# Half-size products of gate and up: four raw weight buffers for two, nine split pairs for ten, six ordinary pairs in front

## The chip, the core and the metric

The kernel runs on one core of a Trainium2 chip. The metric is device time in microseconds (us) of one execution; before the change it is 1347.97 us, the median of three runs (1345.63 to 1348.08).

## What is computed

Two transformer blocks, one after the other, on 512 tokens of 1024 features in float32. The change lies in the feed-forward part of the first block:

```python
h = rms_norm(x, ln_pre_ffn[l])
f = (jax.nn.silu(h @ w_gate[l]) * (h @ w_up[l])) @ w_down[l]
x = x + rms_norm(f, ln_post_ffn[l])
```

`w_gate` and `w_up` are 1024 x 2816 each, `w_down` is 2816 x 1024. Ahead of it stands a mixing layer (dilated attention and pooling), behind it the second block with another mixing layer, a second feed-forward part and a gated output.

## The kernel before

**Split operands.** TensorE (PE) multiplies in a reduced-precision form of float32 (fp32r). To keep accuracy every operand is split in two: `hi` is a rounded copy, written by ScalarE (ACT), and `lo` is what the rounding left, value minus `hi`, written by VectorE (DVE). `mm3` (L185) then makes three matmuls of each product: hi by hi (L188), hi by lo of the other side (L189), lo by hi (L190). A split weight tile of 128 x 512 is a *split pair* (`wh`, `wl` in the profile); `NW` = 10 of them exist. Weights come from memory by DMA, issued by SP, into *raw* buffers (`wr`, up to 128 x 1048 float32); the pool `wts` (L71) holds two.

**The pairs.** Gate and up are made in 22 pairs of output blocks, 128 gate columns and the 128 up columns beside them. The first `PLAIN` = 5 pairs are ordinary: each block is a slab of 8 k-tiles x 3 matmuls with 512 columns (tokens), so 48 matmuls a pair. The other 17 pairs are made by Strassen's scheme in Winograd's form: the weights of a pair are four pieces (gate and up, each with an upper and a lower half of the 1024 features), the activations four quarters (two feature halves, two token halves), and seven half-size products do for eight. A half-size product is 4 k-tiles x 3 matmuls of 256 columns, so a pair takes 84 matmuls of 256. The price is preparation.

- *Of the activations, once:* `h_forms` (L719) makes seven operands out of the four quarters: scaled quarters (L738), sums and differences (L747), and the split of each (L177, L178, L180, L181). These are 15 steps, run after ordinary pair 1, 2 and 3, five at a time (L660 to L665).
- *Of the weights, per pair:* `w_forms` (L762) loads the two raw tiles (L767), makes four sums (L774) and splits seven operands (ACT at L782, DVE at L783).

In the half-size loop (L669 on) the products are named by their number j: 0 to 4 are made in the pair's turn, 5 (`left`) and 6 (`right`) are put off into the next pair's turn. DVE combines the results: L693 needs product 3, L697 needs 4, L701 needs 5, L705 needs 6; L707 and the split at L180/L181 finish the activation.

**What sets the order.** The code names dependencies only; the instructions of each engine are put in their order when the program is built, by a planner that plays the program on a model of the engines. On the chip each engine then runs its queue in that order, and waits by semaphores. So a change of buffer counts alters the order everywhere. A tile whose buffer is in use waits for the last reader of the tile before it: a raw tile for the last ACT or DVE operation that reads it, a split pair for the last matmul.

Of the kernel before, what the change touches and what calls it, by code (L numbers as in the profile page):

```python
# [26 lines left out]
GATE = 5  # L27
GATE2 = 4
WARM = 10
NW = 10  # L30
BANKS = (3, 2, 2, 1)
SHARE = 4
ORDER1 = (
# [9 lines left out]
DONE2 = [0, 1, 2, 3, 4, 5, 6, 7]  # L43
KA2 = 6
BESIDE = 4
PLAIN = 5
NA2 = 4
SLOTS = dict(h=16, o=14, k=16, z=6, v=8, p=8, t=6, m=8)

# [13 lines left out]
class Builder:  # L63
    def __init__(self, ctx, tc, io):
        self.tc = tc
        self.nc = tc.nc
        self.io = io
        self.n = 0
        pool = lambda name, bufs, **k: ctx.enter_context(tc.tile_pool(name=name, bufs=bufs, **k))
        self.cp = pool("const", 1)  # L70
        self.wp = pool("wts", 2)  # L71
        self.sp = pool("slots", 1)
        self.mp = pool("small", 8)
        self.dp = pool("dram", 1, space=bass.MemoryType.DRAM)
        psum = dict(space=bass.MemoryType.PSUM)
        self.pd = pool("psd", BANKS[0], **psum)
        self.pS = pool("pss", BANKS[1], **psum)
        self.pT = pool("pst", BANKS[2], **psum)
        self.pV = pool("psv", BANKS[3], **psum)
        self.cyc = 0  # L80
        self.nlo = 0
        self.share = 0
# [68 lines left out]
    def wunit(self, name, u, parts=2, pieces=1):  # L151
# [9 lines left out]
        for i in range(parts):  # L161
            c = raw[:, i * w:i * w + w]
            hi = self.wp.tile([P, WH], F32R, tag="hi", name=self.nm("wh"), bufs=NW)
            lo = self.wp.tile([P, WH], F32R, tag="lo", name=self.nm("wl"), bufs=NW)
            nc.scalar.activation(hi[:, :w], c, AF.Copy)  # L165
# [466 lines left out]
    def ffn1(self, h, R):  # L632
        nc = self.nc
        self.tables("silu_and_others")
        get = self.units("w_gu1")
        self.parked = self.dp.tile([KD, P, S], F32, tag="parked", name="parked")
        for m in range(KD):
            nc.sync.dma_start(self.parked[m], self.res[m])
        act = []
        todo = []  # L640
        for i in range(PLAIN):
            if i == 0:
                early = [self.psum(True) for _ in range(BESIDE)]
                self.beside(early, range(BESIDE), h, ((0, 256), (256, S)), get)
            gu = []
            for s in (2 * i, 2 * i + 1):
                if s < BESIDE:
                    gu.append(early[s])
                    continue
                gu.append(self.psum(True))  # L650
                self.slab(gu[-1], "w_gu1", s, h, units=get)
            g, u = gu
            t = self.slot("z")
            nc.vector.tensor_tensor(t, g, R, ALU.mult)
            self.act(t, t, AF.Silu)
            w = self.slot("z")
            nc.vector.tensor_tensor(w, u, R, ALU.mult)
            nc.vector.tensor_tensor(t, t, w, ALU.mult)
            act.append(self.split(t, **self.act_tiles1(i)))
            if i == 0:  # L660
                forms, todo = self.h_forms(R)
                each = -(-len(todo) // (PLAIN - 2))
            else:
                for step in todo[(i - 1) * each:i * each]:
                    step()  # L665
        self.res = None
        sums = [self.slot("m") for _ in range(4)]
        late = []
        for i in range(PLAIN, KF):  # L669
            wf = self.w_forms(2 * i, sums)  # L670
            A, B, C = (self.psum(True) for _ in range(3))
            half = slice(0, 256)
            e, f, t = self.slot("z"), self.slot("z"), self.slot("z")

            def times(out, j, first=False, wf=wf):
                hi, lo = wf(j)
                for k in range(4):
                    c = slice(k * P, k * P + P)
                    a = slice(k % 2 * 256, k % 2 * 256 + 256)
                    bh, bl = forms[j][k // 2]  # L680
                    self.mm3(out[:, half], hi[:, c], lo[:, c], bh[:, a], bl[:, a], first and k == 0, k == 3, True)

            times(A, 0, True)
            nc.scalar.activation(e[:, half], A[:, half], AF.Copy)
            times(C, 1, True)
            for step in late[:1]:
                step()
            times(A, 2)
            nc.scalar.activation(e[:, 256:], A[:, half], AF.Copy)
            for step in late[1:]:  # L690
                step()
            times(B, 3, True)
            nc.vector.tensor_tensor(t[:, half], B[:, half], e[:, half], ALU.add)  # L693
            self.act(t[:, half], t[:, half], AF.Silu)
            times(A, 4)
            nc.scalar.activation(f[:, half], A[:, half], AF.Copy)
            nc.vector.tensor_tensor(f[:, 256:], C[:, half], f[:, half], ALU.add)  # L697

            def left(A=A, t=t, times=times):
                times(A, 5)  # L700
                nc.vector.tensor_tensor(t[:, half], t[:, half], A[:, half], ALU.mult)  # L701

            def right(C=C, t=t, e=e, f=f, times=times, i=i):
                times(C, 6)
                nc.vector.tensor_tensor(t[:, 256:], C[:, half], e[:, 256:], ALU.add)  # L705
                self.act(t[:, 256:], t[:, 256:], AF.Silu)
                nc.vector.tensor_tensor(t[:, 256:], t[:, 256:], f[:, 256:], ALU.mult)  # L707
                act.append(self.split(t, -1.0, **self.act_tiles1(i)))
            late = [left, right]
        for step in late:  # L710
            step()
        self.tables("natural_log_exp_and_others")
        return self.post(act, None, "w_down", "ln_post_ffn", "ln_mix_2", False)
# [48 lines left out]
    def w_forms(self, u, sums):  # L762
# [15 lines left out]
        for j, f in enumerate(src):  # L778
            c = f()
            hi = self.wp.tile([P, WH], F32R, tag="hi", name=self.nm("wh"), bufs=NW)  # L780
            lo = self.wp.tile([P, WH], F32R, tag="lo", name=self.nm("wl"), bufs=NW)
            nc.scalar.activation(hi[:, :512], c, AF.Copy)  # L782
# [423 lines left out]
```

## Time and profile before

| | us |
|---|---|
| median of three runs | 1347.97 |
| the profiled execution's own time | 1350.33 |
| its span (first to last instruction) | 1348.5 |
| PE busy in the span | 1302.2 |
| DVE busy | 937.3 |
| ACT busy | 724.0 |
| POOL busy | 153.5 |

The page gives busy time per engine, the span in 40 slices, and the chain of work that ended last, followed backwards from the last instruction. The trace behind it can be asked for single stretches: busy time and granted clock of TensorE in a window, the instructions in order of time, and who waited for whom. A matmul's duration in the trace is longer than the distance to the next, since matmuls overlap; what a stream of them costs is read from start to start. Below, the half-size stage is the stretch from 295.68 us (first half-size matmul) to 485.04 us (first matmul of `w_down`).

### The profile page before, as it was taken

Reading aid. Unit: us, or ns where it says so; the run is one execution under the profiler, and the core shown is the slowest. Engines: PE = TensorE matmul, PEld = TensorE weight load, DVE = VectorE, ACT = ScalarE, POOL = GpSimd, SP = SyncE. Lnnn points to the kernel's source line nnn. Section 1 sums busy time; section 2 is a strip of 40 time slices with the busy share of each in tenths; the row PEclk is TensorE's granted clock in tenths of the full one; section 3 lists DMA queues with packets and bytes.
Section 4 is the critical chain, followed back from the end, with each engine's and each line's share of the span. In section 5 each row is a group of like instructions: output and inputs, shape, how many; then the busy total and the mean of one; then the engine's idle time right before and its main releaser. Section 6 shows DMA issues by size and latency. Waiting matters only on the chain.

```text
span 1348.5 us, 21638 instructions
## 1 busy us (share of the span) xinstructions
PE 1302.2 (97%) x8062; PEld 1156.7 (86%) x8062; DVE 937.3 (70%) x1962; ACT 724.0 (54%) x1460; POOL 153.5 (11%) x190
## 2 busy tenths in 40 slices
PE   9799999989999999999999999999999999999998
PEld 9799979868999988888989999788888888888887
DVE  6777985898888863228688878766887777733354
ACT  6466745655555653227577777754554444522241
POOL 1233320000000000001223334430000000000000
PEclk9999999999999999999999999999999999999999
DMA  6322333412222363227334444224322222222221
GB/s 226 113 63 68 95 103 117 135 38 95 95 95 95 102 212 110 94 78 224 129 106 117 124 115 137 79 95 150 115 97 97 99 96 94 102 94 94 94 79 63
DMA packets 51114, 145.99 MB, mean 108 GB/s; under 512 B 6497, under 2 KB 7393, under 8 KB 51009
## 3 DMA queue, kind: packets, MB, share of 16 engines
q1 hardware_dynamic: 51008, 144.62, 33.4%
q8 instruction: 63, 1.03, 0.3%
q14 instruction: 43, 0.34, 0.1%
HBM read 124.47 MB, written 8.39 MB: 99 GB/s over the span
## 4 chain that ended last, share of the span: by engine, by line
PE 69%; DVE 20%; DMA 7%; issue 2%; ACT 2%; SPq 0%; POOL 0%; DVEq 0%; ACTq 0%; POOLq 0%
PE p L188 16%; PE p L190 16%; PE p L189 16%; DMA wr<-in_w_gu 5%; PE p L374 5%; PE p L375 5%; PE p L376 4%; DVE wl L783 4%; DVE sm L774 3%; DVE wl L168 2%; PE p L285 2%; PE p L294 1%; PE p L293 1%; PE p L263 1%; DVE sp L267 1%
## 5 line engine op out<-in xcount | busy, mean ns | idle before, releaser
L168 DVE TENSOR_TENSOR wl<-wr,wh 128x512 fp32r<-128x512 f32 x332 | 237.4, 727 | 200.6 <-ACT wh L165 193.3
L165 ACT ACTIVATE wh<-wr 128x512 fp32r<-128x512 f32 (+1 forms) x349 | 215.8, 629 | 294.4 <-PE p L189 237.6
L188 PE MATMUL p<-sh,wh 128*128 128x512 f32 (+1 forms) x768 | 260.3, 343 | 10.7 <-ACT wh L782 10.1
L190 PE MATMUL p<-sh,wl 128*128 128x512 f32 (+1 forms) x768 | 263.9, 345 | 2.9 <-DVE wl L783 2.4
L189 PE MATMUL p<-sh,wh 128*128 128x512 f32 (+1 forms) x768 | 261.3, 342 | 0.0
L374 PE MATMUL p<-wh,sh 128*128 128x256 f32 (+1 forms) x672 | 193.2, 289 | 6.8 <-ACT sz L488 3.8
L375 PE MATMUL p<-wl,sh 128*128 128x256 f32 (+1 forms) x672 | 191.8, 286 | 0.2
L376 PE MATMUL p<-wh,sh 128*128 128x256 f32 (+1 forms) x672 | 190.9, 286 | 0.0
L188 PEld LDWEIGHTS p<-sh,wh 128*128 128x128 f32 x768 | 144.3, 189 | 31.1 <-ACT wh L782 12.5
L190 PEld LDWEIGHTS p<-sh,wl 128*128 128x128 f32 x768 | 145.7, 190 | 24.4 <-DVE wl L783 6.4
L189 PEld LDWEIGHTS p<-sh,wh 128*128 128x128 f32 x768 | 145.6, 190 | 18.2 <-issue 0.2
L374 PEld LDWEIGHTS p<-wh,sh 128*128 128x128 f32 x672 | 128.7, 192 | 9.9 <-ACT sz L488 4.0
L375 PEld LDWEIGHTS p<-wl,sh 128*128 128x128 f32 x672 | 128.9, 192 | 1.1 <-DVE wl L168 0.7
L376 PEld LDWEIGHTS p<-wh,sh 128*128 128x128 f32 x672 | 128.2, 191 | 1.3 <-issue 0.5
L189 PE MATMUL p<-sk,wh 128*128 128x512 f32 (+1 forms) x274 | 95.1, 354 | 0.1
L190 PE MATMUL p<-sk,wl 128*128 128x512 f32 (+1 forms) x274 | 95.2, 354 | 0.0
L275 POOL TENSOR_SCALAR sp<-sp,m 128x128 f32<-128x128 f32 (+1 forms) x112 | 71.0, 638 | 185.0 <-DVE m L271 147.4
L113 ACT ACTIVATE sp<-sp,m 128x128 f32<-128x128 f32 (+3 forms) x128 | 71.5, 559 | 35.8 <-DVE m L267 33.3
L188 PE MATMUL p<-sk,wh 128*128 128x512 f32 (+1 forms) x274 | 88.3, 354 | 1.9 <-ACT sk L177 1.4
L188 PE MATMUL p<-so,wh 128*128 128x512 f32 (+1 forms) x246 | 88.5, 364 | 0.6 <-DVE m L267 0.5
L189 PE MATMUL p<-so,wh 128*128 128x512 f32 (+1 forms) x246 | 89.1, 362 | 0.0
L190 PE MATMUL p<-so,wl 128*128 128x512 f32 (+1 forms) x246 | 88.9, 362 | 0.0
(250 smaller groups left out, 2677.4 us busy)
## 6 DMA issues: line engine op xcount, KB each, us to landing
wr<-in_w_gu SPq DMA_DIRECT2D x88, 512.0 KB
wr<-in_w_down SPq DMA_DIRECT2D x44, 512.0 KB
wr<-in_w_qk SPq DMA_DIRECT2D x31, 512.0 KB
sk<-sk SPq DMA_DIRECT2D x88, 128.0 KB
wr<-in_w_out SPq DMA_DIRECT2D x12, 512.0 KB
sv<-in_x SPq DMA_DIRECT2D x16, 256.0 KB
wr<-in_w_ple_gate SPq DMA_DIRECT2D x8, 512.0 KB
wr<-in_w_v SPq DMA_DIRECT2D x6, 512.0 KB
```

Of the source, the lines that this page charges most:

```text
L113: i = self.nc.scalar.activation(out, in_, func, **k)
L165: nc.scalar.activation(hi[:, :w], c, AF.Copy)
L168: eng.tensor_tensor(lo[:, :w], c, hi[:, :w].bitcast(F32), ALU.subtract)
L188: mm(out, lhsT=ahi, rhs=bhi, start=start, stop=False, **more)
L189: mm(out, lhsT=ahi, rhs=blo, start=False, stop=False, **more)
L190: mm(out, lhsT=alo, rhs=bhi, start=False, stop=stop, **more)
L275: self.nc.gpsimd.tensor_scalar(p[:, :n], p[:, :n], m[:, 2:3], 1.0, ALU.mult, ALU.mult)
L374: mm(d, lhsT=h[k][0][:, a], rhs=hi[:, c], start=k == 0 and (o == 0 or not first), stop=False)
L375: mm(d, lhsT=h[k][0][:, a], rhs=lo[:, c], start=False, stop=False)
L376: mm(d, lhsT=h[k][1][:, a], rhs=hi[:, c], start=False, stop=k == 7 and (o > 0 or not first))
L774: nc.vector.tensor_tensor(out, a, b, ALU.add)
L783: nc.vector.tensor_tensor(lo[:, :512], c, hi[:, :512].bitcast(F32), ALU.subtract)
```

## The change

The raw pool holds four buffers instead of two; `NW` is 9 instead of 10; `PLAIN` is 6, so six pairs are ordinary and 16 are made by half-size products. The 15 preparation steps are dealt out over `PLAIN - 1` = 5 ordinary pairs, three after each of pairs 1 to 5, instead of five after each of three. The parameter `dynamic_dma_scratch_size`, an area for descriptors of DMAs that the program makes itself, goes from 2048 to 512.

```diff
-NW = 10
+NW = 9
-PLAIN = 5
+PLAIN = 6
...
-        self.wp = pool("wts", 2)
+        self.wp = pool("wts", 4)
...
             if i == 0:
                 forms, todo = self.h_forms(R)
-                each = -(-len(todo) // (PLAIN - 2))
+                each = -(-len(todo) // (PLAIN - 1))
...
     nc = bacc.Bacc("TRN2", target_bir_lowering=False, num_devices=1,
-                   dynamic_dma_scratch_size=2048)
+                   dynamic_dma_scratch_size=512)
```

The order of the queues moves with it. First, DVE's queue in the middle of the half-size stage, about one pair's worth. Before, where `wl882` to `wl888` are the operands 0 to 3 of the next pair, `sz876` is the current pair's result and `sz852` the one before it:

```order
L693 TENSOR_TENSOR sz876_4080<-p872_4076,sz874_4078 128x256
L181 SCALAR_TENSOR_TENSOR st878_4148<-sz852_3940,st877_4147 128x512
L783 TENSOR_TENSOR wl882_4184<-wr879_4179,wh881_4183 128x512
L774 TENSOR_TENSOR sm805_3787<-wr880_4181 128x512
L774 TENSOR_TENSOR sm807_3789<-wr879_4179,wr880_4181 128x512
L697 TENSOR_TENSOR sz875_4079<-p873_4077,sz875_4079 128x256
L774 TENSOR_TENSOR sm806_3788<-sm805_3787,wr879_4179 128x512
L783 TENSOR_TENSOR wl884_4189<-sm805_3787,wh883_4188 128x512
L774 TENSOR_TENSOR sm808_3790<-sm806_3788,wr879_4179 128x512
L701 TENSOR_TENSOR sz876_4080<-sz876_4080,p871_4075 128x256
L783 TENSOR_TENSOR wl886_4194<-sm806_3788,wh885_4193 128x512
L783 TENSOR_TENSOR wl888_4198<-wr879_4179,wh887_4197 128x512
```

The same place of the queue now. `wl1090` to `wl1098` are operands 0 to 4 of one pair (raw tiles `wr1087`, `wr1088`), `sm821` on `wr1112` is the first sum of the pair after it, and `sz1084`, `sz1060`, `sz1036` are results of the three pairs before `wl1090`'s:

```order
L783 TENSOR_TENSOR wl1090_5384<-wr1087_5379,wh1089_5383 128x512
L697 TENSOR_TENSOR sz1059_5139<-p1057_5137,sz1059_5139 128x256
L774 TENSOR_TENSOR sm824_3870<-sm822_3868,wr1087_5379 128x512
L783 TENSOR_TENSOR wl1092_5389<-sm821_3867,wh1091_5388 128x512
L693 TENSOR_TENSOR sz1084_5280<-p1080_5276,sz1082_5278 128x256
L181 SCALAR_TENSOR_TENSOR sk1062_5208<-sz1036_5000,sk1061_5207 128x512
L783 TENSOR_TENSOR wl1094_5394<-sm822_3868,wh1093_5393 128x512
L701 TENSOR_TENSOR sz1060_5140<-sz1060_5140,p1055_5135 128x256
L774 TENSOR_TENSOR sm821_3867<-wr1112_5521 128x512
L783 TENSOR_TENSOR wl1096_5398<-wr1087_5379,wh1095_5397 128x512
L783 TENSOR_TENSOR wl1098_5403<-sm823_3869,wh1097_5402 128x512
L705 TENSOR_TENSOR sz1060_5140<-p1057_5137,sz1058_5138 128x256
```

What moved: before, operand 0 of the next pair stands behind L693 and L181 of the running one; now operands 0 and 1 of a pair stand ahead of L693 of the pair before it, and sums of one pair are made among the splits of another, which takes raw tiles of two pairs at once.

Second, PE's queue where the half-size stage begins. Before: the end of the first product (`wh811`), and the first matmuls of the next two:

```order
L190 MATMUL p825_3827<-sh719_3467,wl812_3796 128x256
L188 MATMUL p827_3829<-sh723_3475,wh813_3800 128x256
L189 MATMUL p827_3829<-sh724_3476,wh813_3800 128x256
L188 MATMUL p825_3827<-sh747_3573,wh815_3805 128x256
L189 MATMUL p825_3827<-sh748_3574,wh815_3805 128x256
L190 MATMUL p827_3829<-sh723_3475,wl814_3801 128x256
```

Now, 60 matmuls into the stage: product 4 of the first half-size pair ends (`wl836`), and operands 0, 1 and 3 of the second pair are begun with their hi parts, before the first use of a lo part (`wl850`):

```order
L190 MATMUL p841_3907<-sh787_3749,wl836_3895 128x256
L188 MATMUL p863_4015<-sh717_3463,wh849_3983 128x256
L189 MATMUL p863_4015<-sh718_3464,wh849_3983 128x256
L188 MATMUL p865_4017<-sh739_3555,wh851_3988 128x256
L189 MATMUL p865_4017<-sh740_3556,wh851_3988 128x256
L188 MATMUL p864_4016<-sv811_3847,wh855_3997 128x256
L189 MATMUL p864_4016<-sv812_3848,wh855_3997 128x256
L190 MATMUL p863_4015<-sh717_3463,wl850_3984 128x256
```

What moved: the second pair's operand 0 is wanted before products 5 and 6 of the first pair are made, 66 matmuls after the stage began.

Third, DVE's queue ahead of that `wl850`; here `wl836` to `wl840` belong to the first half-size pair, `wr847` and `wr848` are the raw tiles of the second, and `sz781`, `sz807` are the activations of the last two ordinary pairs:

```order
L783 TENSOR_TENSOR wl836_3895<-sm823_3869,wh835_3894 128x512
L774 TENSOR_TENSOR sm821_3867<-wr848_3981 128x512
L783 TENSOR_TENSOR wl838_3899<-wr826_3873,wh837_3898 128x512
L658 TENSOR_TENSOR sz807_3837<-sz807_3837,sz808_3840 128x512
L774 TENSOR_TENSOR sm824_3870<-sm822_3868,wr825_3871 128x512
L178 TENSOR_TENSOR st784_3742<-sz781_3735,st783_3741 128x512
L774 TENSOR_TENSOR sm823_3869<-wr847_3979,wr848_3981 128x512
L774 TENSOR_TENSOR sm822_3868<-sm821_3867,wr847_3979 128x512
L178 TENSOR_TENSOR st810_3844<-sz807_3837,st809_3843 128x512
L783 TENSOR_TENSOR wl840_3904<-sm824_3870,wh839_3903 128x512
L693 TENSOR_TENSOR sz846_3912<-p842_3908,sz844_3910 128x256
L783 TENSOR_TENSOR wl850_3984<-wr847_3979,wh849_3983 128x512
```

What moved: sums of the second pair now stand between the splits of the first, along with the last steps of the ordinary pairs. From the first L654 of ordinary pair 0 to this `wl850` DVE's queue holds 81 operations: 64 of 512 columns, 16 scaled quarters (L738) and one L693. Before, from the same L654 to `wl816` (operand 2 of the first half-size pair), it holds 64: 48 of 512 columns and the 16 quarters.

## Rows read from the trace of the kernel before

**Rows 1.** The page: chain by line, and DMA queue (packets, MB, share)

```profile
PE p L188 16%; PE p L190 16%; PE p L189 16%; DMA wr<-in_w_gu 5%; PE p L374 5%; PE p L375 5%; PE p L376 4%; DVE wl L783 4%; DVE sm L774 3%; DVE wl L168 2%; PE p L285 2%; PE p L294 1%; PE p L293 1%; PE p L263 1%; DVE sp L267 1%
...
q1 hardware_dynamic: 51008, 144.62, 33.4%
```

**Rows 2.** Busy time, instructions (x) and granted clock (PEclk) in stretches

```profile
core 0: us, PE busy (x) PEld busy (x) DVE busy (x) ACT busy (x) POOL busy (x), PEclk, DMA share, GB/s
314.07:476.22 162.15, 155.74 (x1266) 150.90 (x1265) 137.64 (x256) 94.35 (x195) 0.00 (x0) 0.99 0.30 98
455.00:464.00 9.00, 9.00 (x79) 9.00 (x77) 8.38 (x17) 6.00 (x12) 0.00 (x0) 1.00 0.34 110
1000.00:1100.00 100.00, 100.00 (x433) 81.06 (x432) 72.59 (x109) 48.75 (x73) 0.00 (x0) 1.00 0.28 95
295.68:485.04 189.36, 175.94 (x1405) 169.82 (x1404) 162.68 (x300) 108.82 (x224) 0.00 (x0) 0.96 0.29 94
...
299.70:309.90 10.20, 5.39 (x24) 4.86 (x23) 10.20 (x19) 4.71 (x8) 0.00 (x0) 0.50 0.02 6
368.00:371.30 3.30, 3.30 (x17) 3.30 (x17) 2.86 (x6) 2.50 (x6) 0.00 (x0) 0.50 0.00 0
0.00:207.00 207.00, 194.31 (x1376) 181.18 (x1377) 159.00 (x382) 127.91 (x278) 54.61 (x79) 0.98 0.37 114
600.00:895.00 295.00, 282.17 (x2083) 263.13 (x2082) 233.68 (x655) 206.42 (x492) 95.18 (x109) 0.99 0.42 123
```

**Rows 3.** Chain that ended last, around one half-size pair (start us, us, what)

```profile
454.59 1.29 DVE sm L774 x2
455.89 0.33 DVE sz L697
...
461.12 3.96 DMA wr<-in_w_gu
...
465.10 1.29 DVE sm L774 x2
```

**Rows 4.** PE in order of time, first and last half-size products (start us, us; idle before)

```profile
295.68 0.28 PE L188 MATMUL p<-sh,wh 128*128 128x256 f32 x1
...
296.99 0.28 PE L190 MATMUL p<-sh,wl 128*128 128x256 f32 x1
299.36 0.39 PE L188 MATMUL p<-sh,wh 128*128 128x256 f32 x1 [2.09 <-ACT wh L782]
...
304.63 0.58 PE L188 MATMUL p<-sh,wh 128*128 128x256 f32 x1 [4.73 <-ACT wh L782]
...
485.04 0.50 PE L188 MATMUL p<-sp,wh 128*128 128x512 f32 x1
```

**Rows 5.** DVE in order of time, from the end of the norm's factor on

```profile
270.53 0.69 DVE L238 SCALAR_TENSOR_TENSOR sm<-sz,sm 128x512 f32<-128x512 f32 x1
271.64 0.69 DVE L168 TENSOR_TENSOR wl<-wr,wh 128x512 fp32r<-128x512 f32 x1 [0.41 <-ACT wh L165]
272.25 0.68 DVE L654 TENSOR_TENSOR sz<-p,sm 128x512 f32<-128x512 f32 x1
...
274.64 3.25 DVE L738 SCALAR_TENSOR_TENSOR so<-sv,cols,sm 128x256 f32<-128x256 f32 x8
277.81 0.69 DVE L654 TENSOR_TENSOR sz<-p,sm 128x512 f32<-128x512 f32 x1
...
288.41 1.29 DVE L178 TENSOR_TENSOR sh<-so,sh 128x512 fp32r<-128x512 f32 x2
289.61 0.69 DVE L747 TENSOR_TENSOR so<-so,so 128x512 f32<-128x512 f32 x1
...
307.44 0.68 DVE L783 TENSOR_TENSOR wl<-sm,wh 128x512 fp32r<-128x512 f32 x1
```

**Rows 6.** Groups of instructions from 314.07 to 476.22 (count | busy us, mean ns)

```profile
L782 ACT ACTIVATE wh<-sm 128x512 fp32r<-128x512 f32 x60 | 37.5, 625 | 30.5 <-DVE sm L774 30.5
```

**Rows 7.** Waits of PE from 0 to 207 us (total us, times, longest)

```profile
PE p L263 <- DMA sk<-sk: 1.2, 1, 1.2
```

## The prediction

> **What bounds the kernel now.** I read the chain first. Nearly half of it is the ordinary split products (L188 to L190), which is PE at work; what stands out is 5% in DMAs of `w_gu`, 4% in L783 and 3% in L774 [rows 1], all three lines of the half-size stage. So the question is what that stage costs beyond its matmuls.
>
> What matmuls cost is read where PE has no gap. From 1000 to 1100 us 433 matmuls of 512 columns touch a window of 100.00 us; two of these lie across its edges, so one costs 100/431 = 0.232 us. From 455 to 464 us 79 of 256 columns touch 9.00 us: 9.00/77 = 0.117 us [rows 2]. An ordinary pair is then 48 x 0.232 = 11.14 us, a half-size pair 84 x 0.117 = 9.83 us. The 17 half-size pairs want 167.1 us; the stage took 189.36 us [rows 2, 4]. 22.3 us are lost, in two ways.
>
> - *At the start.* The first product runs from 295.68 to 296.99 us; then PE stands for 2.09 and for 4.73 us, each time for a split weight (ACT `wh`) [rows 4]. DVE is busy all the while (10.20 of 10.20 us from 299.70 on), and the granted clock is at 0.50, the lower level of 1.2 GHz, for these 10.2 us [rows 2].
> - *In every pair.* From one L774 of a pair to the same of the next it is 162.15/15 = 10.81 us [rows 2], 0.98 more than the matmuls. The chain of waits shows a closed ring: sums and splits of a pair, a DMA of 3.96 us, the sums of the next, 10.51 us from 454.59 to 465.10 [rows 3]. With two raw buffers the next pair's weights can't be fetched while this pair's are still read. DVE itself is busy 137.64/15 = 9.18 us a pair, ACT 6.29 [rows 2].
>
> The Trainium skill (Perfetto Trace Analysis, Identifying the Most-Contended Engine) says that matmul busy time is no good measure of what PE has left, and the share of weight loads a better one. By matmul busy time the 15 pairs leave 162.15 - 155.74 = 6.4 us to win, by weight loads 162.15 - 150.90 = 11.3, by start-to-start distances 14.7. I go by the last; the first would put the gain in the 16 pairs at 6.8 us in place of 15.7.
>
> **Part by part.**
>
> *Four raw buffers.* A pair's raw tiles are now fetched while the pair before is split. The 3.96 us leave the ring, and what is left of it, 10.81 - 3.96 = 6.85 us, is below PE's 9.83. What is late next: DVE with 9.18 us, ACT with 6.29, both below 9.83, so PE. But DVE's queue is in order, and in it stand L693, L697, L701 and L705, which wait for PE. Before, operand 0 of the next pair stands two places behind L693 of the running one, and PE wants it as soon as the running pair ends. Now operands 0 and 1 stand ahead of that L693, and behind it only operands wanted about a pair later: between L705 of one pair and the next first use of an operand behind it lie 30 or more matmuls (3.5 us) more than the DVE work between them needs. So I cost these waits at nothing; if the cover is gone, see the slower rival. The two DMAs of a pair move 1 MB in 9.83 us, about 107 GB/s; they moved 98 before and 110 in the densest stretch [rows 2]. They are queued on SP behind other raw loads only.
>
> *Nine split pairs.* A pair needs seven, and products 5 and 6 are put off, so a running pair, two late operands and the first two of the next must fit in nine. In PE's new order at least 44 matmuls (5.1 us) lie between the last use of a split pair's buffer and the first use of its successor. Refilling takes ACT's 0.63 [rows 6] and DVE's 0.68 [rows 5]. Taken as nothing; bounds: nothing, and the slower rival's 1.31 us a pair.
>
> *A sixth ordinary pair.* 11.14 - 9.83 = +1.31 us on PE. In return DVE has 11.14 us more for the activations' preparation before the stage begins, which now begins at 295.68 + 11.14 = 306.82 us.
>
> *How late DVE is then.* On DVE, back to back, an operation of 512 columns costs 0.60 us (288.41 to 289.61 for two), a scaled quarter 0.40 (274.64 to 277.81 for eight) [rows 5], a 256-column combination 0.34 [rows 3]. Test on before: 48 and 16 from L654 at 272.25 give 272.25 + 28.8 + 6.4 = 307.45 for operand 2; it started at 307.44 [rows 5]. Now to `wl850`, operand 0 of the second half-size pair: 64 x 0.60 + 16 x 0.40 + 0.34 = 45.1 us. L654 starts at about 272.3: two splits stand between it and L238 (270.53 [rows 5]) in place of one, and the wait of 0.4 us that lay there was for a raw tile. So it starts at 317.4 and ends at 318.1. PE wants it 66 matmuls into the stage, at 306.82 + 66 x 0.117 = 314.5. Late: 3.6 us, of which a little shows earlier, at operand 2 (DVE 310.6, PE 310.0). The same sum for every later operand gives less, and from the fifth pair on DVE is ahead, since it gains 9.83 - 9.18 a pair. So PE stands about 3.7 us in all, not 7. Bounds: nothing, and before's 6.8 us and 10.2 us of low clock.
>
> *Clock.* At 0.50 for 3.3 us, with PE busy, half of the time is lost [rows 2]: 1.7 us. I count one such stretch behind the remaining stall.
>
> *Spreading the steps* is in the DVE sum. *The scratch area:* the page lists no DMAs but hardware-issued ones and instruction fetches [rows 1]: nothing.
>
> *The other stages.* Their order changes too. PE idles 12.7 us of the first 207 and 12.8 us from 600 to 895 [rows 2], and no raw weight is among the long waits there, so more buffers win little. In the first stage raw loads now stand ahead of the row copies (L420) in SP's queue; with four buffers such a load waits for a buffer that is two loads longer free, so I cost it at nothing; PE's longest wait for a copy was 1.2 us [rows 7]. The unknown is bounded by two low-clock stretches more or fewer, 3.4 us, plus small stalls: 4 us either way; I take 0. The stages of `w_down` and the second feed-forward part have PE without gaps.
>
> *The sum.* The stretch from 295.68 to the first matmul of `w_down`: 11.14 + 16 x 9.83 + 3.7 + 1.7 + 0.3 (the last handover, as before) = 174.1 us, against 189.36: -15.2 us. From the profiled execution's own 1350.33 that is 1335.1. The median of the runs shown is 2.4 us below that execution, so 1333 us.
>
> **Rivals.**
>
> - *PE never waits.* If DVE starts its preparation a little sooner (it idled for raw tiles ahead of L654) the 3.7 and the 1.7 us go: 1327 to 1328. For: the DMA waits there vanish. Against: L654 waits for the norm's factor, which hangs on PE.
> - *Late operands linger.* The start costs what it cost before, or in-order waits on DVE keep about a third of the 0.98 us: 4 to 6 us more, 1337 to 1339. For: DVE is at 9.18 of 9.83, and it is 2 to 3 us behind until the fourth pair.
> - *The ring stays.* If raw tiles are not freed or fetched a pair ahead (SP's queue, or the sums that now need two pairs' tiles at once), a pair stays at 10.81: 11.14 + 173.0 + 5.7 = 189.8, 0.4 more than before: 1348, no change. That is also the case in which the change doesn't do what it says. Against: the new queue makes sums of a pair ahead, which needs the tiles there, and 16 fetches of 4 us fit in 9.8.
> - *Slower: one refill a pair.* If in each pair one operand finds all nine split pairs taken until the product just ahead of it ends, PE stands for ACT and DVE one after the other: 0.63 + 0.68, about 1.35 us with the handovers. 16 x 1.35 = 21.6, net +6.4: 1354. It is decided at 15.2/16 = 0.95 us a pair. For: one buffer fewer, and pairs more interleaved, which holds more operands at once. Against: the 44 matmuls above.
>
> **How the numbers follow.** The forecast has 0.60 (1329 to 1336 by itself), PE without waits 0.15, lingering operands 0.14, the ring 0.05, the refill 0.06. About 0.2%, 2.7 us, is what a measurement can tell from no change. The first three are faster, and a little of the ring's spread: 0.90. Same 0.05, slower 0.05. The range 1325 to 1342 holds the first three with the 4 us of the other stages.
>
> **What would show it.** Right: L774 to L774 at 9.8 to 9.9 us; no wait of DVE or ACT for `wr` in the stage; one PE stall of 3 to 4 us about 66 matmuls into it, and none of over 0.3 us later; `w_down` beginning near 470 us. Wrong: a repeated gap in each pair ahead of an L190 (refill) or of a `wh` on fresh raw tiles (ring); the stage as forecast but the total not, which would put the miss in the other stages.

## The result, and the profile after

| | before | after |
|---|---|---|
| median of the timed runs, us | 1346.82 | 1330.44 |
| span of the profiled execution, us | 1348.5 | 1327.0 |
| mean granted clock of TensorE | 0.988 | 0.994 |

The ratio is 0.9879 (95% interval 0.986 to 0.9898): 16.4 us faster, against 15.2 forecast. The time lies 2.6 us below the forecast of 1333, inside its range. The median before is of four runs here; the three that the prediction started from had 1347.97. The two profiled executions differ by more, 21.5 us in their spans, since the one before was 3.5 us above the median of its runs and the one after 1.4 us below.

The chain of waits of the page, by engine and by line, stands against [rows 1]:

```profile
PE 85%; DVE 9%; issue 2%; ACT 2%; POOL 1%; DMA 0%; SPq 0%; DVEq 0%; POOLq 0%; ACTq 0%
PE p L188 21%; PE p L189 21%; PE p L190 21%; PE p L374 5%; PE p L375 5%; PE p L376 5%; PE p L285 2%; PE p L294 1%; DVE wl L168 1%; PE p L263 1%; DVE sp L267 1%; PE p L264 1%; PE p L293 1%; DVE st L178 1%; DVE sh L181 1%
```

The DMA of `w_gu`, L783 and L774, 12% together before, are gone from these lines. What they held is now PE at work: L188 to L190 rose from 48% to 63%.

Busy time, instructions and granted clock in stretches of the kernel after (columns as in [rows 2]); the last row is from the first half-size product to the first matmul of the mixing layer behind `w_down` (L397):

```profile
340.00:440.00 100.00, 100.00 (x852) 100.00 (x851) 93.10 (x176) 63.28 (x132) 0.00 (x0) 1.00 0.33 109
318.18:321.59 3.41, 3.17 (x15) 3.18 (x16) 3.41 (x7) 1.53 (x5) 0.00 (x0) 0.50 0.00 1
306.09:466.91 160.82, 157.78 (x1313) 156.42 (x1311) 148.51 (x275) 101.25 (x210) 0.00 (x0) 0.99 0.35 114
1000.00:1100.00 100.00, 100.00 (x434) 81.13 (x433) 72.64 (x109) 48.89 (x72) 0.00 (x0) 1.00 0.28 95
306.09:604.97 298.88, 295.84 (x1991) 272.19 (x1990) 199.86 (x362) 152.97 (x303) 4.59 (x3) 0.99 0.35 115
```

The same last stretch of the kernel before, which [rows 2] does not have:

```profile
295.68:623.01 327.33, 313.91 (x2075) 284.87 (x2074) 214.38 (x388) 161.99 (x319) 4.21 (x3) 0.98 0.33 110
```

In the middle of the stage PE has no gap: 852 matmuls touch 100.00 us, two of them across its edges, so one costs 100/850 = 0.1176 us and a pair 9.88. The two long stretches hold the same kinds of work and can be set against their matmuls. Before there are 510 of 512 columns and 1564 of 256, which want 510 x 0.232 + 1564 x 0.1176 = 302.2 us, so 25.1 of 327.33 are lost. After there are 510 and 1480, 292.4 us wanted, 6.5 of 298.88 lost. The difference between the spans is 21.5 us: 18.6 of it are this loss, less 1.3 for the sixth ordinary pair, and the rest is ahead of the stage (0.7) and behind L397 (3.5).

PE in order of time at the start of the stage (start us, us; idle before and what ended it), all rows with a gap up to 320 us, and with them the first matmuls of the stage and of `w_down`:

```profile
306.09 0.28 PE L188 MATMUL p<-sh,wh 128*128 128x256 f32 x1
...
309.19 0.39 PE L188 MATMUL p<-sh,wh 128*128 128x256 f32 x1 [1.28 <-ACT wh L782]
...
315.65 0.39 PE L188 MATMUL p<-sh,wh 128*128 128x256 f32 x1 [0.49 <-ACT wh L782]
...
317.52 0.39 PE L188 MATMUL p<-sv,wh 128*128 128x256 f32 x1 [0.84 <-ACT wh L782]
...
318.42 0.58 PE L190 MATMUL p<-sh,wl 128*128 128x256 f32 x1 [0.40 <-DVE wl L783]
...
461.98 0.39 PE L188 MATMUL p<-sp,wh 128*128 128x512 f32 x1
```

Before, two stalls of 2.09 and 4.73 us stood here [rows 4]. Now there are four small ones, and from 319 us to `w_down` no start-to-start distance is more than 0.15 us above a matmul's own. The last products and `w_down` are mixed in PE's queue: after the first two matmuls of `w_down`, at 461.98 us, 36 half-size ones follow; from 466.68 us on it is `w_down`, with 36 half-size ones still in it.

VectorE in order of time: the first L654, the late operand (`wl850` of the planned queue), and the first sums of the third, fourth and last pair:

```profile
272.52 0.68 DVE L654 TENSOR_TENSOR sz<-p,sm 128x512 f32<-128x512 f32 x1
...
317.67 0.69 DVE L783 TENSOR_TENSOR wl<-wr,wh 128x512 fp32r<-128x512 f32 x1
...
322.22 0.68 DVE L774 TENSOR_TENSOR sm<-wr 128x512 f32<-128x512 f32 x1
...
328.27 0.68 DVE L774 TENSOR_TENSOR sm<-wr 128x512 f32<-128x512 f32 x1
...
444.06 0.68 DVE L774 TENSOR_TENSOR sm<-wr 128x512 f32<-128x512 f32 x1
```

One row of ACT, from just ahead of the first stall:

```profile
307.71 0.38 ACT L684 ACTIVATE sz<-p 128x256 f32<-128x256 f32 x1 [2.80 <-PE p L190]
```

And who waited for whom from 330 to 460 us (total us, times, longest), its first three rows:

```profile
ACT wh L782 <- PE p L189: 44.7, 61, 1.5
DVE wl L783 <- ACT wh L782: 4.9, 12, 0.7
DVE sz L705 <- PE p L190: 2.2, 4, 1.0
```

ACT and DVE now wait for PE, that is for buffers and for results; no row of this view, to its end, is a wait for a raw tile.

### The profile page after: what moved, and what is told of

Read it like the earlier page. It is cut to its first block, busy times and chain, and to the rows that moved or that the text cites. A ratio compares the mean times of both kernels' runs of the same rounds, so it can differ in the third digit from the quotient of the medians.

```text
span 1327.0 us, 21696 instructions
## 1 busy us (share of the span) xinstructions
PE 1293.5 (97%) x8026; PEld 1149.7 (87%) x8026; DVE 932.4 (70%) x1953; ACT 718.5 (54%) x1453; POOL 148.7 (11%) x190
## 4 chain that ended last, share of the span: by engine, by line
PE 85%; DVE 9%; issue 2%; ACT 2%; POOL 1%; DMA 0%; SPq 0%; DVEq 0%; POOLq 0%; ACTq 0%
PE p L188 21%; PE p L189 21%; PE p L190 21%; PE p L374 5%; PE p L375 5%; PE p L376 5%; PE p L285 2%; PE p L294 1%; DVE wl L168 1%; PE p L263 1%; DVE sp L267 1%; PE p L264 1%; PE p L293 1%; DVE st L178 1%; DVE sh L181 1%
## 5 line engine op out<-in xcount | busy, mean ns | idle before, releaser
L165 ACT ACTIVATE wh<-wr 128x512 fp32r<-128x512 f32 (+1 forms) x353 | 219.4, 630 | 300.5 <-PE p L189 270.2
L168 DVE TENSOR_TENSOR wl<-wr,wh 128x512 fp32r<-128x512 f32 (+1 forms) x336 | 239.8, 720 | 193.2 <-ACT wh L165 184.1
L188 PE MATMUL p<-sh,wh 128*128 128x512 f32 (+1 forms) x752 | 254.9, 344 | 4.2 <-DVE sv L416 2.4
L189 PE MATMUL p<-sh,wh 128*128 128x512 f32 (+1 forms) x752 | 256.9, 343 | 0.0
L190 PE MATMUL p<-sh,wl 128*128 128x512 f32 (+1 forms) x752 | 254.9, 344 | 0.4 <-DVE wl L783 0.4
L188 PEld LDWEIGHTS p<-sh,wh 128*128 128x128 f32 x752 | 141.1, 189 | 23.1 <-issue 3.0
L189 PEld LDWEIGHTS p<-sh,wh 128*128 128x128 f32 x752 | 142.3, 189 | 18.1 <-issue 0.2
L190 PEld LDWEIGHTS p<-sh,wl 128*128 128x128 f32 x752 | 141.5, 190 | 18.7 <-DVE wl L783 0.6
L374 PEld LDWEIGHTS p<-wh,sh 128*128 128x128 f32 x672 | 127.1, 190 | 7.2 <-ACT sz L488 1.6
L376 PEld LDWEIGHTS p<-wh,sh 128*128 128x128 f32 x672 | 126.9, 189 | 0.7 <-DVE sh L181 0.2
L189 PE MATMUL p<-sk,wh 128*128 128x512 f32 (+1 forms) x290 | 100.7, 356 | 0.3 <-DVE sk L181 0.3
L190 PE MATMUL p<-sk,wl 128*128 128x512 f32 (+1 forms) x290 | 100.9, 356 | 0.0
L188 PE MATMUL p<-sk,wh 128*128 128x512 f32 (+1 forms) x290 | 93.4, 355 | 0.5 <-ACT sk L180 0.3
L188 PE MATMUL p<-so,wh 128*128 128x512 f32 (+1 forms) x246 | 88.0, 361 | 1.4 <-DVE m L267 1.0
L190 PE MATMUL p<-so,wl 128*128 128x512 f32 (+1 forms) x246 | 88.4, 359 | 0.0
```

Of the source, the lines that this page charges most:

```text
L168: eng.tensor_tensor(lo[:, :w], c, hi[:, :w].bitcast(F32), ALU.subtract)
L188: mm(out, lhsT=ahi, rhs=bhi, start=start, stop=False, **more)
L189: mm(out, lhsT=ahi, rhs=blo, start=False, stop=False, **more)
L190: mm(out, lhsT=alo, rhs=bhi, start=False, stop=stop, **more)
L374: mm(d, lhsT=h[k][0][:, a], rhs=hi[:, c], start=k == 0 and (o == 0 or not first), stop=False)
L376: mm(d, lhsT=h[k][1][:, a], rhs=hi[:, c], start=False, stop=k == 7 and (o > 0 or not first))
```

## The experiments

All are edits of the kernel before or after. The table holds, beside the ratio to the kernel before, two readings of each trace: the matmuls that touch 340 to 440 us (850 or more is PE without a gap), and the PE time lost from the first half-size product to L397, worked out as above. R is the number of raw buffers, N of split pairs, P of ordinary pairs. The runs were made in four groups, each with its own runs of the kernel before (medians 1346.82, 1348.37, 1349.16 and 1347.84 us), so kernels of different groups are compared by their ratios. The two readings are of one execution each. PE's gapless rate itself varies a little (850 to 858 in the window), so differences of about 1 us in the last column mean nothing. A half-clock stretch of 3.4 us in the window costs some 14 matmuls: before, e8 and e9 have one there, e3 has 10.2 us of low clock. No run changes the descriptor area (`dynamic_dma_scratch_size`) alone: kernels made from the one after have 512, those made from the one before 2048. The pages before and after list the same three DMA queues, hardware-issued ones and instruction fetches, and no DMA that the program makes itself, so its share is argued to be nothing.

| run | R, N, P | median us | ratio (95%) | matmuls 340-440 | lost us |
|---|---|---|---|---|---|
| before | 2, 10, 5 | 1346.82 | 1 | 774 | 25.1 |
| after | 4, 9, 6 | 1330.44 | 0.9879 (0.986-0.9898) | 852 | 6.5 |
| e1 | 4, 9, 5 | 1333.93 | 0.9893 (0.9872-0.9914) | 851 | 10.8 |
| e2 | 2, 10, 6 | 1340.49 | 0.9935 (0.9911-0.9958) | 790 | 18.2 |
| e3 | 2, 9, 5 | 1351.38 | 1.0026 (1.0008-1.0043) | 739 | 29.8 |
| e4 | 3, 10, 6 | 1329.96 | 0.9864 (0.9843-0.9885) | 855 | 2.3 |
| e5 | 4, 7, 6 | 1321.25 | 0.9805 (0.978-0.9829) | 851 | 3.4 |
| e6 | 4, 9, 6, four steps | 1327.17 | 0.9843 (0.982-0.9866) | 851 | 3.8 |
| e7 | 3, 10, 7 | 1331.96 | 0.9876 (0.9852-0.99) | 850 | 1.4 |
| e8 | 2, 10, 5, half loads | 1338.94 | 0.9936 (0.9915-0.9958) | 805 | 17.1 |
| e9 | 2, 7, 5 | 1342.58 | 0.9961 (0.9946-0.9976) | 782 | 25.0 |
| e10 | 4, 6, 6 | 1332.68 | 0.9882 (0.9868-0.9896) | 858 | 1.4 |
| e11 | 4, 7, 6, four steps | 1323.38 | 0.9817 (0.9803-0.9831) | 851 | 3.4 |
| e12 | 3, 7, 6 | 1324.36 | 0.982 (0.9806-0.9834) | 851 | 3.5 |

**e1: the raw buffers without the sixth pair.**

```diff
-PLAIN = 6
+PLAIN = 5
-                each = -(-len(todo) // (PLAIN - 1))
+                each = -(-len(todo) // (PLAIN - 2))
```

> Four raw buffers and nine split pairs, but five ordinary pairs and five preparation steps after each of three, as before. Theory (the ring is what the raw buffers break; the sixth pair only trades 1.31 us on TensorE for a shorter stall at the start): the half-size pairs run at 9.83 us, but VectorE is one ordinary pair (11.14 us, less some 8 operations of 0.60 us) later at the start, so TensorE stands about 10 us there with some 3 us of low clock; that is about 12 us faster than the kernel before, 1334 to 1337 us, and 4 to 6 us slower than the changed kernel. Rival A (the sixth pair and the spread bring most of the gain): at most 5 us faster than before, 1342 or more. Rival B (the sixth pair costs more than it gives): 1328 to 1330, not slower than the changed kernel.

14.4 us faster than before, as the theory's 12 or so, and rival A falls. Against the kernel after, the theory's 4 to 6 us are not borne out: it is 1.9 us by the ratios, whose intervals overlap, so the total alone does not separate it from rival B. The gap in each pair is gone (851 matmuls), the start is not. PE in order of time, the only gaps in the stage:

```profile
301.99 0.58 PE L188 MATMUL p<-sh,wh 128*128 128x256 f32 x1 [2.60 <-ACT wh L782]
...
307.14 0.58 PE L188 MATMUL p<-sh,wh 128*128 128x256 f32 x1 [4.36 <-ACT wh L782]
```

These are before's two stalls [rows 4] again, with the clock at 0.50 for the same 10.2 us. The first 200 half-size matmuls lose 10.3 us here and 11.1 before. So with five ordinary pairs the start costs about 10.8 us, ring or no ring, and the ring cost before 25.1 - 10.8 = 14.3 us.

**e2: the sixth pair without the raw buffers.** Of the kernel before, with its ten split pairs:

```diff
-PLAIN = 5
+PLAIN = 6
-                each = -(-len(todo) // (PLAIN - 2))
+                each = -(-len(todo) // (PLAIN - 1))
```

> Two raw buffers and ten split pairs as before, but six ordinary pairs with three steps after each of five. Theory: the ring of 10.8 us a pair stays for 16 pairs; the start loses a few us less, the sixth pair costs 1.31 us and takes one ring pair of 0.98 us away: 0 to 5 us faster than before, 1342 to 1347 us, with a 4 us DMA of raw weights in the chain of waits in each pair. Rival A: 10 to 16 us faster, 1331 to 1337. Rival B: 1 us slower than before or more.

8.8 us faster by the ratio, between the theory's 5 and rival A's 10 (the interval, 5.7 to 12.0 us, reaches into the rival's range); the ring is there all the same. The chain of waits around one pair (start us, us, what):

```profile
386.21 4.41 DMA wr<-in_w_gu
390.61 0.02 issue
390.64 1.29 DVE sm L774 x2
391.93 0.34 DVE sz L697
...
396.54 0.61 DVE wl L783
397.15 0.02 issue
397.17 4.50 DMA wr<-in_w_gu
```

10.96 us from DMA to DMA. The gain is at the start: the first 200 half-size matmuls lose 4.4 us where they lost 11.1 before. The whole stretch loses 6.9 us less (0.8 of it for the pair that left the ring) for 1.3 us more of matmuls; the other 3 us lie elsewhere, 2.2 of them ahead of the stage, which begins at 304.6 us against 295.7 + 11.1. The expectation had taken before's start at some 6 us; e1 shows 10.8.

**e3: nine split pairs alone** (`NW = 9` in the kernel before).

> The kernel before with nine split pairs for ten and nothing else. Theory (nine are enough): within 4 us of before, either way, 1343 to 1351 us, the ring at 10.8 us a pair. Rival (each pair waits for a refill, 1.35 us): where the ring hides the refill in its own wait, still no change; where the two add up, up to 1.35 us in each of 17 pairs, 23 us slower, 1370.

3.5 us slower by the ratio, 0.26%, which is more than nothing and far from a refill in each pair. Its profiled execution (1357.54 us) is 6.2 us above the median of its runs, so the 29.8 us lost in its trace are more than usual. Much of the surplus comes from the ring: the two longest gaps of PE behind the start, 2.09 and 2.77 us, each stand behind a DMA of the ring that took longer than the 4.2 us usual before.

```profile
363.83 5.27 DMA wr<-in_w_gu
...
398.84 5.79 DMA wr<-in_w_gu
```

**e4: three raw buffers** (`pool("wts", 3)`, `NW = 10` in the kernel after).

> The changed kernel with three raw buffers and ten split pairs in place of four and nine. Theory: one of a pair's two raw tiles can be fetched a pair ahead, so of the 3.96 us in the ring only what the second tile takes alone stays; 6.85 us plus 3 to 4 is 9.9 to 10.8 us a pair, so 0 to 16 us of the gain are left; likeliest about half, 1335 to 1342 us. Rival (it takes both tiles ahead to get anything): as with two, 1342 to 1347. Rival (one tile ahead is all that it takes): as the changed kernel, 1328 to 1332.

As fast as the kernel after, so the second rival was right and the expectation of half the gain wrong. Set against e2 it is the plainest test of the ring: six ordinary pairs and ten split pairs in both, a third raw buffer here (and the smaller descriptor area). The ratio goes from 0.9935 to 0.9864, whose intervals don't meet, 9.6 us, and the loss from 18.2 to 2.3 us. One buffer more is enough: PE has no gap from 340 to 440 us, and the stage loses even less than in the kernel after, though it begins 2.1 us later.

```profile
340.00:440.00 100.00, 100.00 (x855) 100.00 (x855) 95.62 (x179) 63.70 (x135) 0.00 (x0) 1.00 0.37 117
```

**e5: seven split pairs** (`NW = 7` in the kernel after).

> The changed kernel with seven split pairs for nine. Theory (in TensorE's order 38 or more matmuls of 256 columns, 4.4 us, nearly always lie between the last use of a split pair's buffer and the first use of the next in it, against 1.35 us of refilling): the half-size stage as in the changed kernel, the whole within 4 us of it, 1327 to 1336 us. Rival (one refill a pair decides when the buffers get few): some 1.35 us in each of 16 pairs, 1350 to 1354 us.

Neither theory: 0.74% faster than the kernel after by the two ratios, whose intervals don't meet. No refill is seen: PE has two gaps in the whole stage.

```profile
309.09 0.39 PE L188 MATMUL p<-sh,wh 128*128 128x256 f32 x1 [0.76 <-ACT wh L782]
...
315.24 0.38 PE L188 MATMUL p<-sv,wh 128*128 128x256 f32 x1 [0.47 <-ACT sz L696]
```

Of the 7.7 us between the two spans 3.1 are in the stage and its `w_down`, and 5.0 behind L397 (722.0 us in the kernel after, 717.0 here), less half a microsecond ahead. Of those 5.0, PE's gaps make 2.8 (8.7 us in all there, 11.5 in the kernel after), and 1.7 are one half-clock stretch of 3.4 us less. There is one half-clock stretch in this trace between the first and the last microseconds, of 3.4 us; before had 10.2 us and six of 3.4. The timed runs show the same: the mean granted clock was 0.994 to 0.998 in the five of e5, 0.991 to 0.995 in the four of the kernel after, and 0.986 to 0.992 in the eleven of the kernel before that ran beside e5. One minus the mean clock, times the span, is 4.2, 9.0 and 14.9 us. So about half of what seven split pairs give, and about a third of what the change under study gives, is less time at the low clock (an estimate from these clocks, too high where PE idled at the low one; where such a stretch lies in the stage, the stage's loss holds it too).

**e6: the preparation over four pairs** (`PLAIN - 2` in the kernel after).

> The changed kernel with the preparation dealt out four steps after each of four ordinary pairs, not three after each of five. Theory (VectorE's lateness at the start is the sum of its work up to the first late operand, wherever the steps stand): within 2 us of the changed kernel, 1328 to 1333 us. Rival (the even spread is what the sixth pair needs): 4 us slower, 1334 or more, with the longer stall at the start.

Not slower, so the rival falls; 0.36% faster by the ratios, but the intervals overlap (0.982 to 0.9866 and 0.986 to 0.9898). The theory's "within 2 us" is neither shown nor refuted: the median is 3.3 us lower, in another group of runs. In the trace the stage loses 2.7 us less and begins 2.2 us later.

**e7: a seventh ordinary pair**, on e4.

> Three raw buffers, ten split pairs, seven ordinary pairs with three steps after each of five. The kernel with three buffers and six pairs loses 3.2 us of TensorE time in the stage; a seventh pair costs 1.31 us. Theory (little is left to win at the start): 0 to 1.5 us slower than with six, 1329 to 1333 us. Rival (each further pair wins what the sixth did, some 4 us): 1326 us or less.

1.6 us slower than e4 by the ratios, inside their intervals, and about the theory's sum: 0.9 us less lost in a stage that begins 1.0 us later than the pair alone would have it, and 1.3 us more of matmuls.

**e8: half the bytes.** In `w_forms` of the kernel before:

```diff
-            nc.sync.dma_start(t[:, :KD * P], self.io["w_gu1"][j])
-            raw += [t[:, 0:512], t[:, 512:1024]]
+            nc.sync.dma_start(t[:, :512], self.io["w_gu1"][j][:, :512])
+            raw += [t[:, 0:512], t[:, 0:512]]
```

> The kernel before, two raw buffers; of each raw tile of the half-size pairs only the first 512 columns are loaded, and the second half of the features is replaced by the first, so the output is not the reference's; the number of sums, splits and matmuls is the same. Theory (the DMA of 3.96 us stands in the ring and scales with its bytes): some 1.5 to 2 us less in the ring of 10.5 us, so TensorE's 9.83 us bounds the pair: 0.5 to 1 us a pair, 8 to 15 us faster than before, 1333 to 1340 us. Rival (a fixed latency, or the ring is VectorE's and the DMA only lies beside it): within 4 us of before.

8.6 us faster, at the lower edge of the theory: the DMA stands in the ring. The chain of waits, three pairs:

```profile
390.23 3.32 DMA wr<-in_w_gu
393.57 1.29 DVE sm L774 x2
...
400.70 2.86 DMA wr<-in_w_gu
403.59 1.29 DVE sm L774 x2
...
410.72 3.02 DMA wr<-in_w_gu
...
420.90 3.95 DMA wr<-in_w_gu
```

A pair takes (420.90 - 390.23)/3 = 10.2 us in place of 10.8, so the ring still bounds it and not PE, as the theory had it. The DMA scales less than expected: of the 14 DMAs in before's chain the median is 4.2 us, of the 9 here 3.0. Half the bytes take 1.2 us off, so about 1.8 of the 4.2 us don't depend on bytes (estimate from these two medians). The Trainium skill (DMA: Bandwidth & Descriptors, Anatomy of one DMA) gives a fixed cost of about 2 us for a DMA that GpSimd issues. The DMAs here are issued by SP; that the estimate comes out near it is a likeness, and no run here tests it.

**e9: seven split pairs alone**, in the kernel before.

> The kernel before with seven split pairs for ten and nothing else. The changed kernel became 9 us faster with seven for nine. Theory A (fewer split pairs give an order that starts the half-size stage later in need and idles less elsewhere, whatever the raw buffers): 5 to 9 us faster than before, 1339 to 1344 us. Theory B (that gain was the order's chance in that one setting; here the ring of 10.8 us a pair stays and hides the rest): within 4 us of before, 1344 to 1352. Rival (refills, with no raw tiles ahead): slower, 1355 or more.

5.3 us faster by the ratio, at the lower edge of theory A; the interval, 3.2 to 7.3 us, reaches into theory B's 4. In the stage nothing changed (25.0 us lost); the time came from ahead of the stage (3.3 us in the profiles) and from behind L397 (725.5 us before, 720.1 here). That is 8.7 us between two executions, more than the medians' difference.

**e10: six split pairs**, in the kernel after.

> The changed kernel with six split pairs for nine, fewer than the seven operands of a pair. In TensorE's order some 28 to 38 matmuls of 256 columns (3.3 to 4.4 us) lie between the last use of a buffer and the first use of the next in it. Theory (3.3 us cover a refill of 1.35 us): within 4 us of the kernel with seven, 1317 to 1325 us. Rival (here the refill begins to show, as ScalarE's and VectorE's queues are in order): 5 to 20 us slower than with seven, 1326 to 1341.

10 us slower than e5 by the ratios, as the rival's number said. In the stage it is not by the rival's mechanism: the stage and `w_down` lose 1.4 us, no more than in any other version, and PE has no gap in the middle.

```profile
340.00:440.00 100.00, 100.00 (x858) 100.00 (x857) 94.40 (x176) 64.53 (x134) 0.00 (x0) 1.00 0.33 110
```

The miss is elsewhere: 723.8 us behind L397 against 717.0 in e5, and another 6.8 ahead of the stage, less the 2.0 that its stage loses less. Outside the stage PE idles 31.5 us against 22.8 in e5, and the clock is low for 16.9 us against 5.8. Only 1.3 us of that idle time (0.3 in e5) end when a split weight arrives. But the rival's mechanism is not refuted there, because ACT and DVE run their queues in order. At least one stall hangs on a refill: ACT waits for PE to free a buffer, DVE's split waits for ACT, an operation on activations (L298) stands behind that split, and PE waits for it. What such waits cost in all is not shown.

```profile
184.05 0.63 ACT L165 ACTIVATE wh<-wr 128x512 fp32r<-128x512 f32 x1 [1.48 <-PE p L189]
...
184.71 0.69 DVE L168 TENSOR_TENSOR wl<-wr,wh 128x512 fp32r<-128x512 f32 x1 [1.95 <-ACT wh L165]
185.44 0.69 DVE L298 TENSOR_TENSOR so<-p,st 64x512 f32<-64x512 f32 x1
...
186.28 0.47 PE L293 MATMUL p<-st,sv 128*128 128x512 f32 x1 [0.84 <-DVE so L298]
```

**e11 and e12: e5 with four steps, and e5 with three raw buffers.**

> The changed kernel with seven split pairs and the preparation dealt out four steps after each of four ordinary pairs: the two edits that each made it faster (9 and 3 us) together. Theory (they add where they touch different stalls): 1317 to 1321 us. Rival (the second has nothing left to win: with seven pairs the stage loses 2.9 us in all): 1320 to 1324.

> Three raw buffers, seven split pairs, six ordinary pairs, three steps after each of five: less memory than the kernel before. Theory (three buffers break the ring as four do): within 4 us of the kernel with four and seven, 1318 to 1325 us. Rival (with fewer split pairs the sums are made later, raw tiles are held longer and the ring is back): 1326 or more.

e11 is not faster than e5 (0.9817 and 0.9805, overlapping): the rival. e12 keeps the gain with less memory than the kernel before: one raw buffer of 1048 columns more, three split pairs of two 524-column tiles each fewer. In its trace DVE does wait for raw tiles now and then (3.2 us from 330 to 440 us), without a gap on PE. e5, e11 and e12 all beat both kernels; the three ratios' intervals overlap, and e5's median, 1321.25 us, is the lowest.

## Why the prediction was right, step by step

- *The ring.* Right. With more raw buffers a pair falls from 10.81 us to PE's own 9.88 (forecast 9.83), no one waits for `wr`, and DVE is 93% busy without delaying PE. e1, e2 and e8 show it from three sides, and e2 against e4 with the raw buffer as the only change beside the descriptor area. The size was a little off: the prediction took 0.98 us a pair for it, 16.7 in 17 pairs; e1 against before gives 14.3, or 12.6 for 15 pairs, between the 11.3 by weight loads and the 14.7 by start-to-start distances, and far from the 6.4 by matmul busy time. (Its remark that 16 fetches of 4 us fit in 9.8 is wrong as it stands: a pair makes two.)
- *Why four.* Not worked out. The prediction took the four as given, and its queue holds raw tiles of two pairs at once. e4 and e12 show that three buffers do, each in its own order; with three, one tile at most can be ahead of the two in use.
- *Nine split pairs at nothing.* Right for refills in the stage, down to six, fewer than the seven operands of a pair: e10's stage has almost no loss. So the 44 matmuls that the prediction counted were more cover than needed there, and the slower rival with its refill a pair is refuted. But the number isn't free: alone in the kernel before, nine cost 3.5 us and seven gave 5.3; in the kernel after seven gave 10 more, and all but some 3 us of that outside the stage. The bound was "nothing, and 1.31 us a pair"; the stages outside it were given 4 us either way.
- *The sixth pair.* It saves more than the prediction had in its working. The start cost 10.8 us before (e1), which the prediction's own figures nearly give (2.09 + 4.73 us of stalls, and half of the 5.39 us that PE was busy at the low clock, 9.5 in all), but its split of the 22.3 us left the start only 5.6. With two raw buffers the pair is worth 8.8 us (e2); with four, after against e1, about 2, which the intervals don't separate from nothing.
- *How late DVE is.* The operand was forecast to start at 317.4 us and started at 317.67; L654 at 272.3, and it was 272.52. The stall was forecast as one of 3.7 us about 66 matmuls into the stage. PE stood four times, 3.0 us, and with the handovers lost 4.4. Three of the waits (0.49, 0.84 and 0.40 us) are 60 to 66 matmuls in, the last for `wl850`. The first, of 1.28 us, is 14 matmuls in, and DVE is not its cause: ACT's queue had L684 ahead of the splits, and ACT idled 2.80 us until the first product was done. The prediction looked for such in-order waits on DVE alone. DVE has no idle time there and the 66th matmul waits for its operand in any case, so this wait moved a part of the stall forward and changed the sum little (argued; no run takes L684 away).
- *Clock.* One stretch of 3.41 us at 0.50 behind the stalls, as forecast, 1.7 us.
- *The sum for the stage.* Wrong in its count of matmuls. The first matmul of `w_down` was forecast for 469.8 us and began at 461.98, but this is no like-for-like end: 72 half-size matmuls run after it, 24 before the change. The prediction counted none of the 24, so its 22.3 us lost were 25.1, and its 174.1 us hold 2.8 us of matmuls that the 189.36 beside them do not. With the count put right its own terms give 18.0 us for the stage. Measured up to L397, where this plays no part, it is 25.1 - 6.5 - 1.3 = 17.3: the 5.7 us that it left for the new stage (3.7, 1.7 and 0.3) were 6.5.
- *Other stages.* Costed at 0 with 4 either way. The profiles show 0.7 us ahead and 3.5 behind, 4.2 in all, at the edge. Two half-clock stretches of 3.4 us fewer outside the stage (three after, five before, the last microseconds left out) are 3.4 of it at half speed, the very unknown that the prediction bounded. Before's profiled execution was 3.5 us above the median of its runs and after's 1.4 below, so much of this may be between executions. By the medians the whole is 1.2 us more than forecast, and with the count put right it would be 1.6 us less: if the stage gave 17.3 us in the other executions too, the rest gave nothing. So that 15.2 and 16.4 are so near says little about how well the single stages were costed.
- *A sign misread.* L774 to L774 was to be 9.8 to 9.9 us. It is (444.06 - 328.27)/12 = 9.65: DVE, late at the start, catches up with PE, so its clockwork is not PE's. The matmuls of a window (9.88 us a pair) are the reading that holds.

What stays open: which places of the order make seven split pairs faster, and six slower again, outside the half-size stage. The traces show where in time it happens, that the stage's waits are not the cause, and that idle time of PE and time at the low clock both move; no run moved a single stretch of the order by itself, and none separates the order from in-order waits of ACT and DVE for a buffer.

## What to carry to other kernels

When a chain of waits closes on itself (buffer, DMA, work, buffer), set its length beside the busiest engine's time for one turn; the difference times the turns is the most that a buffer more can give there, and one buffer more may do, so try the smallest step. Count what runs on either side of a mark before two stretches that end at it are set against each other. Read a stage's loss from matmuls per window, not from the distance of another engine's operations. Where a planner makes the order, buffer counts for which no matmul is seen to wait still move the time elsewhere, here by 10 us between nine and seven split pairs: sweep them, downwards too, and look at the granted clock of every run beside its time.

## What was not expected of the hardware

- Half the bytes of a raw DMA took 3.0 us in place of 4.2 (medians of 9 and 14), so halving the transfers did not open the ring: a pair still took 10.2 us (e8).
- Stalls can be paid a second time through the clock. In e1 gaps of 2.60 and 4.36 us came with 10.2 us at 0.50; the lost time was 10.8 us, not 7. In the changed kernel gaps of 3.0 us in all came with 3.4 us at 0.50. It is not so each time: in e10 a gap of 0.76 us at the start of the stage came with no low clock there.
